# Global attention: latent and context scores of a head in one probability buffer

## Chip, cores and metric

The kernel runs on one core of a Trainium2 chip. The metric is device time in microseconds of one execution, as the median of several. PE is TensorE, DVE is VectorE, ACT is ScalarE, POOL is GpSimd, SP is SyncE. PSUM is the memory that PE writes its products to (eight banks of 512 float32 columns), SBUF the on-chip working memory.

## What is computed

One layer of a backbone over 1024 latent tokens (width 1024) and 256 context tokens. Two attention branches work side by side, each with 8 query heads and 2 key/value heads of 64 columns: a windowed branch (each block of 128 queries sees three blocks of keys, the context, and a sink logit) and a global branch (all 1024 latent keys and the 256 context keys). A gated merge and a convolutional feed-forward part follow. What the change touches is the global branch's softmax:

```python
def _global_attention(q, k_all, v_all):
    ...
    def one_block(i):
        q_blk = lax.dynamic_slice_in_dim(q, i * BLOCK, BLOCK, axis=1)
        p = jax.nn.softmax(_gqa_scores(q_blk, k_all), axis=-1)
        return _gqa_values(p, v_all)
...
o_b = _global_attention(q_b, jnp.concatenate([k_b, k_b_c], axis=1), jnp.concatenate([v_b, v_b_c], axis=1))
```

So each query has one softmax over 1024 + 256 = 1280 keys.

## The kernel before

The attention stage works through 32 **units**. A unit is one branch, one block of 128 queries and one key/value head with its four query heads; units 0 to 15 are windowed, 16 to 31 global. Each unit has *score steps* and, one unit later, *value steps*: while unit u's scores are made, the values of unit u-1 are made. The loop at lines 833 to 863 lays both lists out on a scale from 0 to 1 (the score steps over the first 0.85, the value steps over all of it) and calls them in that order. In units 18 to 25 a third list, *fill*, is spread among them: groups of twelve products of the windowed branch's output projection (`branch_steps`, line 792), each of which takes a transpose slot. This order is that of the source. A list planner then fixes each engine's queue: an earlier instruction goes first, but one whose buffer isn't free yet is passed by later ones that are ready.

A global unit before the change:

- `context`/`cxp` (line 464): PE computes the context scores of all four heads, 4 x 256 columns, into one score buffer. DVE takes their maxima (line 471) and scales them (472). ACT takes four exponentials of 256 columns out of PSUM into one probability buffer `p_x` (line 476, through `soft`, 426).
- `lat(h)` for each head (line 428): four products of 512 columns into a score buffer. One DVE instruction (line 459) scales the 1024 scores, writes them negated to the head's probability buffer and keeps the running minimum, which starts from the context's maximum. ACT takes the exponential in place, with the sum.
- `norm` (line 479): the context exponentials were taken with the context's maximum alone, so they are brought to the common one. DVE forms a difference (483), ACT its exponential (484), POOL multiplies the four slices of `p_x` (487), DVE corrects the sums (488, 489) and takes the reciprocal (494).
- Value steps (line 523): for each of ten key tiles of 128, PE transposes the four heads' 128 columns into one transpose slot (531). ACT writes the rounded high part (`pth`, 540) and DVE the rest (`ptl`, 541), or, for tiles 2 and 6, ACT copies the tile out (537) and POOL splits it (line 538, through 84 and 87). PE then multiplies with the values (552, 553), some tiles later. Key tiles 8 and 9 are the context (`pslice`, 518). The output goes through ACT (558), POOL (560, 566) and DVE (563).
- `qprep` (397) prepares the queries of unit u+2 and `rows` (496) the row of reciprocals; each takes a transpose slot for a short time.

Buffers: two score buffers of two banks (`s_tile`, 765), three transpose slots of one bank (`pt_tile`, 762), one bank for the value sums, and eight probability buffers of 1024 columns (`p_tile`, 768). A windowed unit uses four of the eight, a global unit five. A buffer is free again when the last instruction that reads it is done.

The lines that order the steps, and the loop that places them:

```python
        def score_steps(self):
            steps = [lambda h=h: self.lat(h) for h in range(4)]
            return steps + [self.norm]
...
            steps = [lambda n=n: step(range(n, n + g)) for n in range(0, len(kt), g)]
            steps.insert(2 - self.br, self.rows)
...
        for lst, of, sp in ((ss, 0.0, SPAN[u >= 17]), (vs, VOFF, VSPAN), (fs, 0.0, 1.0)):
            for n, st_ in enumerate(lst):
                seq.append((of + sp * (n + 0.5) / len(lst), st_))
        for _, st_ in sorted(seq, key=lambda e: e[0]):
            st_()
```

Of the kernel before, what the change touches and what calls it, by code (L numbers as in the profile page):

```python
# [13 lines left out]
P = 128  # L14
# [55 lines left out]
def layer_kernel(  # L70
# [313 lines left out]
    class Unit:  # L384
# [43 lines left out]
        def lat(self, h):  # L428
# [29 lines left out]
            p = p_tile(f"p{self.id}_{h}")[:, 0:T if self.br else self.w + NC]  # L458
            nc.vector.tensor_scalar(out=p, in0=o, scalar1=self.qscale(nqs)[:, hs] if self.br else -1.0,  # L459
                                    scalar2=self.other[:, hs], op0=ALU.mult, op1=ALU.min, accum_out=self.nm[:, hs])  # L460
            self.soft(p, p, h, self.nm, self.sm, -1.0)
            self.pc[h, 0] = p

        def cxp(self):
            kh = self.br * 2 + self.g
            s = s_tile(f"s{self.id}_x")
            for h in range(4):
                self.qk(s[:, h * NC:(h + 1) * NC], h, KC[0][:, kh])
            self.other = small(f"nmc_{self.id}", (P, 4))
            self.smc = small(f"smc_{self.id}", (P, 4))  # L470
            nc.vector.reduce_max(self.other, s.rearrange("p (a b) -> p a b", a=4), axis=AX.X)
            nc.vector.tensor_tensor(out=self.other, in0=self.other, in1=self.qscale(nqs), op=ALU.mult)
            p = p_tile(f"p{self.id}_x")
            for h in range(4):
                self.pc[h, 1] = p[:, h * NC:(h + 1) * NC]
                self.soft(s[:, h * NC:(h + 1) * NC], self.pc[h, 1], h, self.other, self.smc,
                          self.qscale(pqs)[:, h:h + 1])

        def norm(self):
            hc = slice(self.g * 4, self.g * 4 + 4)  # L480
            f = small(f"f_{self.id}", (P, 4))
            if self.br:
                nc.vector.tensor_tensor(out=f, in0=self.nm, in1=self.other, op=ALU.subtract)
                nc.scalar.activation(f, f, AF.Exp)
                for h in range(4):
                    p = self.pc[h, 1]
                    nc.gpsimd.tensor_scalar(out=p, in0=p, scalar1=f[:, h:h + 1], scalar2=0.0, op0=ALU.mult, op1=ALU.add)
                nc.vector.tensor_tensor(out=self.smc, in0=self.smc, in1=f, op=ALU.mult)
                nc.vector.tensor_tensor(out=self.sm, in0=self.sm, in1=self.smc, op=ALU.add)
            else:  # L490
# [18 lines left out]
        def score_steps(self):  # L509
            steps = [lambda h=h: self.lat(h) for h in range(4)]  # L510
            return steps + [self.norm]

        def context(self):
            self.begin()
            if self.br:
                self.cxp()
# [1220 lines left out]
```

## Time and profile before

| | us |
|---|---|
| median of the runs shown (3) | 1586.1 |
| lowest and highest | 1586.05 and 1589.05 |
| span of the profiled execution | 1585.4 |
| windowed units, about | 340 to 470 |
| global units, about | 470 to 770 |

The profile is of one execution, and its times count from the start of the span. The span runs from that execution's first instruction to its last and is all that the profile gives of its time; it lies 0.7 us below the median of the runs. Rows of groups read: line, engine, operation, names written and read, shape, count, then busy time in us and the mean of one in ns, then the engine's idle time before them and what ended it. Rows of the timeline read: start in us, length in us, engine, line, operation; a bracket at the end is the engine's idle time before it. A row of waits reads: who waited for whom, us in all, times, longest. Matmul ends are modelled and overlap the next start, so PE's work is better read from the steps between starts.

### The profile page before, as it was taken

How to read it: one execution, taken by the hardware profiler on the slowest of the kernel's cores; microseconds unless marked ns; L12 is line 12 of the kernel's file. 1: busy time of each engine (PE TensorE's matmuls, PEld its weight loads, DVE VectorE, ACT ScalarE, POOL GpSimd, SP SyncE). 2: the span in 40 equal slices, each digit the busy share in tenths (PEclk: the TensorE clock that was granted, in tenths of full speed). 3: DMA queues.
4: the chain of work that ended last, by engine and by line, in shares of the span. 5: the costliest groups of instructions: out<-in, count | busy, mean ns of one | idle time of the engine just before them, and what ended most of it. 6: DMA issues, size and time to landing. Idle time of an engine off the chain costs nothing.

```text
span 1585.4 us, 22064 instructions
## 1 busy us (share of the span) xinstructions
PE 1528.4 (96%) x7680; PEld 1269.8 (80%) x7680; DVE 1195.6 (75%) x1766; ACT 813.0 (51%) x1443; POOL 753.7 (48%) x731
## 2 busy tenths in 40 slices
PE   6999999999999999999999999999999999999996
PEld 5878788878887887777788898888888888888876
DVE  7797646628888777888674779888888877657886
ACT  5422222448887667688531565444444444435642
POOL 0574302426667556665422554666667764021132
PEclk9999999999999999999999999999999999999998
DMA  9695662322236555531451132333334446996721
GB/s 378 217 313 188 221 217 81 120 80 67 62 104 157 139 127 145 118 73 39 142 186 53 60 101 86 114 107 112 115 106 118 111 113 189 358 273 210 255 94 53
DMA packets 112367, 229.98 MB, mean 145 GB/s; under 512 B 12960, under 2 KB 27808, under 8 KB 112160
## 3 DMA queue, kind: packets, MB, share of 16 engines
q1 hardware_dynamic: 96816, 198.93, 37.6%
q0 software_dynamic: 10400, 20.19, 8.2%
q10 hardware_dynamic: 5040, 9.46, 1.6%
q8 instruction: 60, 0.98, 0.3%
q14 instruction: 51, 0.42, 0.1%
HBM read 177.35 MB, written 65.86 MB: 153 GB/s over the span
## 4 chain that ended last, share of the span: by engine, by line
PE 82%; DVE 6%; ACT 4%; issue 3%; POOL 2%; DMA 2%; ACTq 0%; SPq 0%; DVEq 0%; POOLq 0%
PE ptr L531 5%; PE p L90 4%; PE p L91 4%; PE p L92 4%; PE g L90 3%; PE g L91 3%; PE g L92 3%; PE b L92 3%; PE b L91 3%; PE b L90 3%; PE s L414 2%; PE a L92 2%; PE c L91 2%; PE d L91 2%; PE c L92 2%
## 5 line engine op out<-in xcount | busy, mean ns | idle before, releaser
L541 DVE TENSOR_TENSOR ptl<-ptr,pth 128x512 fp32r<-128x512 f32 x188 | 124.8, 685 | 27.5 <-ACT pth L540 25.2
L531 PE MATMUL ptr<-ident,p 128*128 128x128 f32 x816 | 126.5, 278 | 10.3 <-DVE ptl L541 7.8
L540 ACT CAST pth<-ptr 128x512 fp32r<-128x512 f32 x188 | 106.6, 588 | 56.3 <-PE ptr L531 32.7
L87 DVE TENSOR_TENSOR ld<-rd,hd 128x1024 fp32r<-128x1024 f32 x77 | 94.0, 1240 | 52.5 <-ACT hd L82 50.4
L426 ACT ACTIVATE p<-p,nm 128x1024 f32<-128x1024 f32 (+2 forms) x128 | 125.3, 981 | 10.9 <-DVE p L459 10.1
L531 PEld LDWEIGHTS ptr<-ident,p 128*128 128x128 f32 x816 | 93.8, 140 | 40.3 <-DVE ptl L541 13.5
L82 ACT CAST hd<-rd 128x1024 fp32r<-128x1024 f32 x77 | 79.2, 1050 | 81.5 <-PE p L92 50.0
L552 PE MATMUL av<-pth,VT 128*128 128x512 f32 x236 | 104.6, 443 | 1.0 <-ACT avs L558 0.5
L90 PE MATMUL p<-hd 128*128 128x512 f32 x264 | 103.2, 391 | 0.0
L92 PE MATMUL p<-hd,ld 128*128 128x512 f32 x264 | 102.7, 389 | 0.0
L91 PE MATMUL p<-ld,hd 128*128 128x512 f32 x264 | 102.7, 389 | 0.0
L90 PE MATMUL g<-hh,whg 128*128 128x512 f32 x256 | 99.9, 390 | 0.0
L92 PE MATMUL g<-hh,wlg 128*128 128x512 f32 x256 | 99.7, 389 | 0.0
L91 PE MATMUL g<-hl,whg 128*128 128x512 f32 x256 | 99.6, 389 | 0.0
L553 PE MATMUL av<-ptl,VT 128*128 128x512 f32 x236 | 97.6, 414 | 2.0 <-POOL ptl L87 1.9
L87 POOL TENSOR_TENSOR wlg<-wg,whg 128x512 fp32r<-128x512 f32 x32 | 47.0, 1479 | 109.6 <-ACT whg L82 107.3
L459 DVE TENSOR_SCALAR_CACHE_REDUCE p<-s,cvt,nmc 128x1024 f32<-128x1024 f32 x64 | 84.5, 1340 | 12.3 <-PE s L415 11.8
L414 PE MATMUL s<-KL,q 128*128 128x512 f32 (+2 forms) x192 | 76.0, 396 | 2.9 <-ACT p_x L426 2.0
L188 DVE CUSTOM_DVE_ANT_0 wml<-wml,sc,bmc 128x1024 f32<-128x1024 f32 x32 | 45.0, 1416 | 39.0 <-DMA wml<-in_wmodT_dram 38.6
L84 POOL TENSOR_SCALAR pth<-prw 128x512 fp32r<-128x512 f32 x48 | 31.1, 649 | 88.2 <-ACT prw L537 62.7
L82 ACT CAST wS<-s 128x512 fp32r<-128x512 f32 x76 | 45.3, 621 | 52.1 <-POOL s L1079 51.3
L415 PE MATMUL s<-KL,q 128*128 128x512 f32 (+2 forms) x192 | 71.7, 373 | 0.0
(396 smaller groups left out, 4974.0 us busy)
## 6 DMA issues: line engine op xcount, KB each, us to landing
wml<-in_wmodT_dram SPq DMA_DIRECT2D x48, 512.0 KB
ru<-in_w_up_dram SPq DMA_DIRECT2D x38, 512.0 KB
rd<-td SPq DMA_DIRECT2D x55, 256.0 KB
rd<-sd SPq DMA_DIRECT2D x44, 256.0 KB
rd<-in_w_dn_dram SPq DMA_DIRECT2D x33, 256.0 KB
wm<-in_wmodT_dram SPq DMA_DIRECT2D x16, 512.0 KB
wg<-in_w_g_dram SPq DMA_DIRECT2D x32, 256.0 KB
sgd<-sg ACTq DMA_DIRECT2D x32, 256.0 KB
```

The lines of the kernel that those rows point to most:

```text
L82: nc.scalar.copy(hi, src)
L87: lo_eng.tensor_tensor(out=lo, in0=src, in1=hi.bitcast(F32), op=ALU.subtract)
L90: nc.tensor.matmul(ps, a[0], b[0], start=start, stop=False, skip_group_check=resumed)
L91: nc.tensor.matmul(ps, a[0], b[1], start=False, stop=False, skip_group_check=resumed)
L92: nc.tensor.matmul(ps, a[1], b[0], start=False, stop=stop, skip_group_check=resumed)
L414: nc.tensor.matmul(o, self.q[0][:, hs], ks, start=True, stop=False)
L426: nc.scalar.activation(p, s, AF.Exp, bias=nm[:, h:h + 1], scale=scale, accum_out=sm[:, h:h + 1])
L531: nc.tensor.transpose(tr[:, h * P:(h + 1) * P], self.pslice(h, n), ident)
L540: nc.scalar.copy(hi, tr)
L541: nc.vector.tensor_tensor(out=lo, in0=tr, in1=hi.bitcast(F32), op=ALU.subtract)
L552: nc.tensor.matmul(self.av, v, hi, start=first, stop=False)
L553: nc.tensor.matmul(self.av, v, lo, start=False, stop=self.left == 0)
```

## The change

In the global branch the context scores of a head go behind its 1024 latent ones, in a probability buffer of 1280 columns. `cxp` runs twice for a unit, for heads 0 and 1 ahead of the score steps and for heads 2 and 3 between the second head's and the third head's step. Each time it computes two heads' context scores into one transpose slot (instead of a score buffer). For each head a DVE instruction then scales the 256 scores, writes them negated to columns 1024 to 1279 and keeps their minimum. `lat` starts its minimum from that and writes the first 1024 columns, and one exponential of ACT covers all 1280. The rescaling of the context and the correction of the sums go. There are six probability buffers of 1280 columns instead of eight of 1024; a global unit uses four. In the windowed branch two heads share one buffer, 640 columns each, so a unit uses two.

```diff
--- before.py
+++ after.py
@@ -455,39 +455,32 @@
                 self.qk(s[:, 512:512 + NC], h, KC[0][:, kh])
                 o = s[:, 512 - w:512 + NC]
             hs = slice(h, h + 1)
-            p = p_tile(f"p{self.id}_{h}")[:, 0:T if self.br else self.w + NC]
-            nc.vector.tensor_scalar(out=p, in0=o, scalar1=self.qscale(nqs)[:, hs] if self.br else -1.0,
+            if self.br == 0:
+                if h % 2 == 0:
+                    self.pp = p_tile(f"p{self.id}_{h}").rearrange("p (a b) -> p a b", a=2)
+                self.pc[h] = self.pp[:, h % 2, 0:self.w + NC]
+            p = self.pc[h]
+            nc.vector.tensor_scalar(out=p[:, 0:T] if self.br else p, in0=o, scalar1=self.qscale(nqs)[:, hs] if self.br else -1.0,
                                     scalar2=self.other[:, hs], op0=ALU.mult, op1=ALU.min, accum_out=self.nm[:, hs])
             self.soft(p, p, h, self.nm, self.sm, -1.0)
-            self.pc[h, 0] = p
-
-        def cxp(self):
+
+        def cxp(self, a):
             kh = self.br * 2 + self.g
-            s = s_tile(f"s{self.id}_x")
-            for h in range(4):
-                self.qk(s[:, h * NC:(h + 1) * NC], h, KC[0][:, kh])
-            self.other = small(f"nmc_{self.id}", (P, 4))
-            self.smc = small(f"smc_{self.id}", (P, 4))
-            nc.vector.reduce_max(self.other, s.rearrange("p (a b) -> p a b", a=4), axis=AX.X)
-            nc.vector.tensor_tensor(out=self.other, in0=self.other, in1=self.qscale(nqs), op=ALU.mult)
-            p = p_tile(f"p{self.id}_x")
-            for h in range(4):
-                self.pc[h, 1] = p[:, h * NC:(h + 1) * NC]
-                self.soft(s[:, h * NC:(h + 1) * NC], self.pc[h, 1], h, self.other, self.smc,
-                          self.qscale(pqs)[:, h:h + 1])
+            s = pt_tile(f"s{self.id}_x{a}")
+            if a == 0:
+                self.other = small(f"nmc_{self.id}", (P, 4))
+            for h in (a, a + 1):
+                self.qk(s[:, (h - a) * NC:(h - a + 1) * NC], h, KC[0][:, kh])
+            for h in (a, a + 1):
+                p = self.pc[h] = p_tile(f"p{self.id}_{h}")
+                nc.vector.tensor_scalar(out=p[:, T:NK], in0=s[:, (h - a) * NC:(h - a + 1) * NC],
+                                        scalar1=self.qscale(nqs)[:, h:h + 1], scalar2=3.0e38, op0=ALU.mult,
+                                        op1=ALU.min, accum_out=self.other[:, h:h + 1])
 
         def norm(self):
             hc = slice(self.g * 4, self.g * 4 + 4)
-            f = small(f"f_{self.id}", (P, 4))
-            if self.br:
-                nc.vector.tensor_tensor(out=f, in0=self.nm, in1=self.other, op=ALU.subtract)
-                nc.scalar.activation(f, f, AF.Exp)
-                for h in range(4):
-                    p = self.pc[h, 1]
-                    nc.gpsimd.tensor_scalar(out=p, in0=p, scalar1=f[:, h:h + 1], scalar2=0.0, op0=ALU.mult, op1=ALU.add)
-                nc.vector.tensor_tensor(out=self.smc, in0=self.smc, in1=f, op=ALU.mult)
-                nc.vector.tensor_tensor(out=self.sm, in0=self.sm, in1=self.smc, op=ALU.add)
-            else:
+            if self.br == 0:
+                f = small(f"f_{self.id}", (P, 4))
                 nc.vector.tensor_tensor(out=f, in0=self.nm, in1=sinkb[:, hc], op=ALU.add)
                 nc.scalar.activation(f, f, AF.Exp)
                 nc.vector.tensor_tensor(out=self.sm, in0=self.sm, in1=f, op=ALU.add)
@@ -508,17 +501,17 @@
 
         def score_steps(self):
             steps = [lambda h=h: self.lat(h) for h in range(4)]
+            if self.br:
+                steps.insert(2, lambda: self.cxp(2))
             return steps + [self.norm]
 
         def context(self):
             self.begin()
             if self.br:
-                self.cxp()
+                self.cxp(0)
 
         def pslice(self, h, n):
-            if self.br and n >= NT:
-                return self.pc[h, 1][:, (n - NT) * P:(n - NT + 1) * P]
-            return self.pc[h, 0][:, n * P:(n + 1) * P]
+            return self.pc[h][:, n * P:(n + 1) * P]
 
         def value_steps(self):
             nm, kt = self.id, self.kt
@@ -766,7 +759,7 @@
         return ps2.tile([P, T], F32, tag="s", name=name, bufs=2)
 
     def p_tile(name):
-        return att.tile([P, T], F32, tag="p", name=name, bufs=8)
+        return att.tile([P, NK], F32, tag="p", name=name, bufs=6)
 
     def small(name, shape):
         return att.tile(list(shape), F32, tag=name.split("_")[0], name=name,
```

## Prediction, made before the change was run

> **What bounds the kernel now.** I read the page first: its span, its engine totals and PE's share of 40 equal slices.
>
> ```profile
> span 1585.4 us, 22064 instructions
> ...
> PE 1528.4 (96%) x7680; PEld 1269.8 (80%) x7680; DVE 1195.6 (75%) x1766; ACT 813.0 (51%) x1443; POOL 753.7 (48%) x731
> ...
> PE   6999999999999999999999999999999999999996
> ```
>
> PE is busy for 96% of the span, and for nine tenths or more of every slice but the first and the last. So an engine beside it matters only where PE waits for it. The change touches the attention stage, so next come the busy times by stretch, cut where a global unit opens. The maximum at line 471 marks that: 16 units, numbered 16 to 31; the rows of the timeline below are those of units 19, 26 and 31.
>
> ```profile
> L471 DVE TENSOR_REDUCE nmc<-s_x x16: 1209/1215/1226, 472.5 to 747.7; 128x4 f32<-128x1024 f32 x16
> ```
>
> ```profile
> 521.61 1.22 DVE L471 TENSOR_REDUCE nmc<-s_x 128x4 f32<-128x1024 f32 x1
> ...
> 665.86 1.22 DVE L471 TENSOR_REDUCE nmc<-s_x 128x4 f32<-128x1024 f32 x1
> ...
> 747.74 1.22 DVE L471 TENSOR_REDUCE nmc<-s_x 128x4 f32<-128x1024 f32 x1
> ```
>
> The busy times by stretch give the length, then the busy microseconds of PE, PE's weight loads, DVE, ACT and POOL:
>
> ```profile
> 472.46:521.61 49.15, 45.52 (x258) 35.65 (x257) 40.38 (x74) 39.34 (x90) 33.98 (x49) 1.00 0.73 171
> 521.61:665.86 144.25, 141.53 (x795) 116.06 (x794) 106.41 (x183) 96.74 (x210) 83.59 (x111) 1.00 0.56 132
> 665.86:764.00 98.14, 90.96 (x533) 72.13 (x531) 86.27 (x146) 80.20 (x180) 57.61 (x83) 1.00 0.23 54
> ```
>
> Units 19 to 25 carry "fill" (the output projection of the windowed branch): 144.25 / 7 = 20.6 us a unit, and PE idles 2.72 us in all, 0.4 a unit. The units from 26 have no fill: (747.74 - 665.86) / 5 = 16.4 us each, and PE idles 98.14 - 90.96 = 7.18 us in six, 1.2 a unit. With the first stretch that makes 13.5 us of idle PE in 291.5. This caps what relief of other engines can give here. What PE waited for in it:
>
> ```profile
> PE ptr L531 <- DVE ptl L541: 7.1, 11, 1.6
> PE s L414 <- ACT p_x L426: 2.0, 3, 0.8
> ```
>
> PE is as full after this stage, so I pass a shift of the stage on to the span in full.
>
> **What goes and what comes, engine by engine.** These groups are the durations that I use.
>
> ```profile
> L459 DVE TENSOR_SCALAR_CACHE_REDUCE p<-s,cvt,nmc 128x1024 f32<-128x1024 f32 x64 | 84.5, 1340 | 12.3 <-PE s L415 11.8
> ...
> L426 ACT ACTIVATE p<-p,nm 128x1024 f32<-128x1024 f32 x64 | 73.8, 1154 | 8.9 <-DVE p L459 8.2
> ...
> L426 ACT ACTIVATE p_x<-s_x,nmc,cvt 128x256 f32<-128x256 f32 x64 | 35.4, 567 | 4.9 <-DVE nmc L472 4.9
> ...
> L487 POOL TENSOR_SCALAR p_x<-p_x,f 128x256 f32<-128x256 f32 x64 | 29.9, 497 | 10.2 <-ACT f L484 10.1
> ...
> L426 ACT ACTIVATE p<-p,nm 128x640 f32<-128x640 f32 x28 | 23.4, 839 | 0.0
> L459 DVE TENSOR_SCALAR_CACHE_REDUCE p<-s,negsink 128x640 f32<-128x640 f32 x27 | 23.1, 874 | 0.2 <-PE s L415 0.2
> ...
> L483 DVE TENSOR_TENSOR f<-nm,nmc 128x4 f32<-128x4 f32 x16 | 7.1, 446 | 0.1
> ...
> L459 DVE TENSOR_SCALAR_CACHE_REDUCE p<-s,negsink 128x512 f32<-128x512 f32 x8 | 5.6, 742 | 0.0
> ...
> L489 DVE TENSOR_TENSOR sm<-sm,smc 128x4 f32<-128x4 f32 x16 | 5.6, 353 | 0.1
> ...
> L488 DVE TENSOR_TENSOR smc<-smc,f 128x4 f32<-128x4 f32 x16 | 4.9, 306 | 2.5 <-ACT f L484 2.5
> ...
> L472 DVE TENSOR_TENSOR nmc<-nmc,cvt 128x4 f32<-128x4 f32 x16 | 4.6, 289 | 0.2
> ```
>
> DVE loses, per unit, the maximum (1.215) and four small operations (0.289 + 0.446 + 0.306 + 0.353): 2.6 us. It gains four reductions of 256 columns out of PSUM, a form that the trace does not have. The 512- and 640-column rows differ by 132 ns for 128 columns, 1.03 ns a column; 742 - 256 x 1.03 = 0.48 us each, as an estimate. The bounds are 0.43 (with the 1.21 ns a column between the 640 and 1024 rows) and the whole 742 of the 512-column row. I take 0.48, since 512 is the nearest row: +1.9, net **-0.7 us a unit** (-0.9 to +0.4).
>
> ACT loses four small exponentials (2.3) and gains 256 columns on each of four large ones. The slope from 640 to 1024 columns is (1154 - 839) / 384 = 0.82 ns, so 0.21 us each, 1364 ns for the new form: net **-1.4 us a unit**. POOL loses the four rescalings, **-2.0**. PE's own work stays: the same eight context products, now in two lots of four. No DMA is issued, removed or moved.
>
> Nothing of this is PE time. The exponential of the context held one of two score buffers; the 2.0 us that PE waited for it go. Of the 7.1 us for DVE's `ptl` I take 1.5, since DVE only loses 0.7 of some 14.4 us a unit (86.27 / 6); the bounds are 0 and 7.1.
>
> Relief in sum: 2.0 + 1.5 = **-3.5 us**, with bounds of 0 and -9.1.
>
> How sure DVE's share is depends on its small operations, which are uneven:
>
> ```profile
> 667.11 2.22 DVE L472 TENSOR_TENSOR nmc<-nmc,cvt 128x4 f32<-128x4 f32 x1
> ```
>
> ```profile
> 666.92 2.40 POOL L87 TENSOR_TENSOR lwb<-rwb,hwb 128x1024 fp32r<-128x1024 f32 x1
> ```
>
> Four elements took 2.22 us while POOL ran a 2.40 us operation. The Trainium skill (SBUF — State Buffer, section "SBUF: two separate sides") says that VectorE and GpSimd share a port pair under an exclusive lock, and that a VectorE operation with two SBUF inputs is blocked for a whole GpSimd instruction; this row agrees. By that rule such stalls leave with the instructions, because the new reductions have one PSUM input, and DVE's net stays at -0.7; if the stalls were chance and moved to DVE's next instruction, the net would be about half of that and the relief nearer -2.8.
>
> **What the change makes wait.** The probabilities lie in a ring of buffers. Before, a unit used five of eight (four heads, one for the context of all). Unit u's first three went in beside the five of unit u-1, and its third and fourth heads needed a head buffer of u-1 back, which the transposes of key tiles 0 to 7 release. The trace shows this hand-over in unit 31:
>
> ```profile
> 757.61 0.60 PE L531 MATMUL ptr<-ident,p 128*128 128x128 f32 x4
> ...
> 757.92 1.34 DVE L459 TENSOR_SCALAR_CACHE_REDUCE p<-s,cvt,nmc 128x1024 f32<-128x1024 f32 x1
> ...
> 759.19 1.34 DVE L459 TENSOR_SCALAR_CACHE_REDUCE p<-s,cvt,nmc 128x1024 f32<-128x1024 f32 x1
> ...
> 759.21 1.03 PE L531 MATMUL ptr<-ident,p_x 128*128 128x128 f32 x8
> ...
> 760.92 1.15 ACT L426 ACTIVATE p<-p,nm 128x1024 f32<-128x1024 f32 x1
> ...
> 762.05 0.83 PE L531 MATMUL ptr<-ident,p 128*128 128x128 f32 x5
> ```
>
> Transposes of tile 7 at 757.61; the third head's reduction 0.3 us later and the fourth behind it; the fourth exponential at 760.92; the next unit's transposes that read it at 762.05, some 4.1 us after the release. In between PE has the transposes of the context tiles (1.03) and products of values and of the next scores, so it hardly idles.
>
> After, a unit uses four of six. The third and fourth heads again wait for u-1, but a buffer now also holds the context columns, which are transposed last (key tiles 8 and 9). So the release comes after **all** transposes of u-1. What follows on DVE and ACT, from the release: two context reductions (2 x 0.40, the busy time less the 0.08 by which the next one starts early), two large ones (2 x 1.27, the step from 757.92 to 759.19), and the last exponential behind the one before it (1.36, and 0.3 for hand-overs): **5.0 us** until the next unit's transposes can finish their first tile. Queued behind those four reductions on DVE are the `ptl` of tiles 8 and 9 and the next unit's first reductions, and PE's value products wait for them.
>
> What PE has to do in these 5 us is priced by the steps from one start to the next: context products, a head's four score products (to the transposes behind them), and value products.
>
> ```profile
> 746.73 0.28 PE L414 MATMUL s_x<-KC,q 128*128 128x256 f32 x1
> 746.84 0.28 PE L415 MATMUL s_x<-KC,q 128*128 128x256 f32 x1
> ...
> 756.03 0.39 PE L414 MATMUL s<-KL,q 128*128 128x512 f32 x1
> ...
> 756.94 0.60 PE L531 MATMUL ptr<-ident,p 128*128 128x128 f32 x4
> ...
> 758.28 0.40 PE L552 MATMUL av<-pth,VT 128*128 128x512 f32 x1
> 758.52 0.40 PE L553 MATMUL av<-ptl,VT 128*128 128x512 f32 x1
> ```
>
> Value products of four tiles are left, 8 x 0.24 = 1.9; the first two heads' context, 4 x 0.12 = 0.5; two heads' scores, 2 x 0.91 = 1.8, each only when DVE has read a score buffer. That is 4.2 us. The gap is 0.8 a unit. Fill groups come too late in the order to cover it and need a transpose slot. Part of the gap falls into the 0.4 to 1.2 us that PE idles already; I take 0.5 for each of 15 units (17 to 31): **+7.5 us**, with bounds of 0 and 15 x 0.9 = +13.5.
>
> Second, the context scores leave the score buffers for the three transpose slots (`pt_tile`). The lot for heads 2 and 3 is computed early (ahead of key tiles 2 and 3) but is only read after the release, so one of three slots is blocked for most of the value tiles. A slot's life is the transposes (0.60 for four, above) and what reads it:
>
> ```profile
> L541 DVE TENSOR_TENSOR ptl<-ptr,pth 128x512 fp32r<-128x512 f32 x167 | 111.0, 685 | 27.4 <-ACT pth L540 25.2 <-POOL O L87 0.8 <-PE av L553 0.5
> ...
> L540 ACT CAST pth<-ptr 128x512 fp32r<-128x512 f32 x164 | 93.2, 588 | 53.1 <-PE ptr L531 29.8 <-PE av L552 20.8
> ```
>
> That is 1.9 us (0.60 + 0.59 + 0.69), and with the queues on ACT and DVE some 2.6, as an estimate. A tile whose split POOL does needs ACT alone, 1.2, and so does the query tile. For key tiles 2 to 9 through two slots that makes (6 x 2.6 + 3 x 1.2) / 2 = 9.6 us. With 0.9 for tiles 0 and 1 (1.03 for eight transposes in the rows above, less the tail) and the 5.0 above, a unit without fill can't be shorter than 15.5. It takes 16.4 now, so I book nothing, but the margin is only 0.9.
>
> Windowed units: two heads share a buffer, six hold twelve heads instead of eight. DVE lost 0.2 us there on scores and nothing on buffers, so I book nothing. If waits went by buffer rather than by columns, each odd head would wait 0.84 us for the even one's exponential, at most 64 / 2 x 0.84 = 27 us; the heads' columns don't overlap, so I leave that out of the range.
>
> Sum: -3.5 + 7.5 = +4.0; span 1589.4. The median of the runs, 1586.1, is 0.7 above the profiled span, so I predict **1590.1 us**.
>
> **Rivals.** *Slots and buffers starve PE (slower by far).* The margin of 0.9 us goes where a slot's life passes 2.9 us, since each 0.1 of life costs 6 x 0.1 / 2 = 0.3 us a unit. At 3.3 a unit takes 17.6, +1.2 in 15 units: +18 us, and +8 to +25 for lives about that. For it: PE waited longest for `ptl` even with three free slots. Against it: ACT and POOL get lighter, and these feed the slots. The Trainium skill (Perfetto Trace Analysis, section "Optimization Strategy") names this case: a gap that repeats through a stretch can mean that the next tile finds no SBUF or PSUM. No run here shows it yet; before, PE idles 0.4 us in a unit with fill.
>
> *The relief wins (faster).* If the list order puts five us of PE work between the release and the next transposes, the chain is hidden as it is now; only the relief stays: -3.5 to -9.1 us, 1577 to 1583, with 1580 in its middle. It decides where at least 0.8 us of products of older tiles or of fill are left at the release. For it: in the hand-over quoted PE hardly idles over 4.1 us. Against it: with fill, PE has only 0.4 us a unit to win back.
>
> *Both cancel.* Within 2 us of before, since PE's own work is the same.
>
> **How the numbers follow.** Forecast (+0.5 to +8, with 0.5 a unit booked for a gap of 0 to 0.9): 0.42. Starved: 0.18. Relief wins: 0.30. Cancel: 0.10. About 0.2% (3.2 us) is what a measurement here can tell from none. Slower by more: 0.27 of the forecast and all of the starved case, 0.45. Faster by more: 0.30. The rest, 0.25, is within it. The range reaches from 1578 (most of the relief case) to 1603 (the starved case but for its end).
>
> **What would show it.** Right: a new DVE form of 128x256 near 0.48 us x64, an ACT form of 128x1280 near 1.36 us, no POOL rescaling; third-head reductions behind the last transposes of u-1; units from 26 on at 16 to 17 us and a PE gap ahead of each unit's first transposes. Wrong: these reductions ahead of the last transposes, or PE waiting for `ptl` by over 15 us in the stage (starved), or PE idle below 10 us in it (relief).

## Result, and the profile after

The change makes the kernel slower: 1609.45 us (four runs, 1607.65 to 1611.09) beside 1586.09 before, a ratio of 1.0132 with an interval of 1.0112 to 1.0152. That is +23.4 us by the medians where +4.0 was forecast, and above the range; by the ratio, which the experiments below go by, it is +20.9 (0.0132 x 1586.1). The direction was right; the time is that of the rival "Slots and buffers starve PE".

Single operations came out as worked out. The page of the changed kernel, its span, totals, PE's slices and groups:

```profile
span 1609.3 us, 21848 instructions
...
PE 1541.5 (96%) x7680; PEld 1267.9 (79%) x7680; DVE 1193.0 (74%) x1814; ACT 792.8 (49%) x1299; POOL 724.1 (45%) x667
...
PE   6999999999999999999899999999999999999996
```

Two groups of it, with shapes kept apart:

```profile
L426 ACT ACTIVATE p<-p,nm 128x1280 f32<-128x1280 f32 x64 | 87.3, 1365 | 26.2 <-DVE p L463 26.0
...
L476 DVE TENSOR_SCALAR_CACHE_REDUCE p<-s_x,cvt 128x256 f32<-128x256 f32 x64 | 28.9, 473 | 10.0 <-PE ptr L524 10.0
```

The long exponential takes 1365 ns (1364 forecast), the reduction of 256 columns 473 ns (480 forecast). POOL loses 29.6 us of 753.7, ACT 20 of 813, DVE only 2.6 of 1195.6. Every engine but PE has less to do, and PE's 7680 products are the same in number. Yet ACT's exponentials now wait 26 us for DVE instead of 8, and DVE's context reductions 10 us for PE's transposes, which are read as the release. One slice of PE falls from 9 to 8.

Busy times by stretch, cut as before (length, then busy PE, weight loads, DVE, ACT, POOL):

```profile
473.13:525.59 52.46, 49.10 (x268) 36.71 (x266) 39.46 (x81) 34.76 (x59) 28.34 (x37) 1.00 0.67 161
525.59:684.46 158.87, 147.56 (x795) 113.69 (x792) 104.36 (x204) 87.16 (x148) 73.97 (x85) 1.00 0.51 121
684.46:785.00 100.54, 92.02 (x522) 69.00 (x520) 81.67 (x163) 72.44 (x125) 43.51 (x56) 1.00 0.22 51
```

The units with fill (second row) take 158.87 / 7 = 22.7 us instead of 20.6. PE idles 11.3 us in that stretch instead of 2.7, and its "busy" time grew by 6 with the same 795 products, since ends are modelled: lengths say more than busy times here. The last value product moved from 774.26 to 797.67, by 23.4 us, and what follows it is as long as before (811.1 and 811.6 us). So the loss lies in the attention stage. Cut from one first-head reduction to another in both kernels, units 19 to 25 take 158.9 us instead of 143.1 (2.3 more each), units 26 to 30, which have no fill, 83.7 instead of 80.6 (0.6 more each), and the last unit up to its last value product 5.3 more.

What PE waited for in all of it, which was 7.1 us for `ptl` and 2.0 for `p_x` before:

```profile
PE s L414 <- DVE p L463: 6.6, 14, 0.6
PE av L546 <- POOL ptl L87: 3.7, 6, 1.2
PE ptr L524 <- DVE ptl L534: 3.2, 9, 0.9
PE ptr L524 <- ACT p L426: 2.0, 1, 2.0
```

The wait for `p_x` is gone and the one for `ptl` is less than half. What has grown most: PE's score products wait 14 times, 6.6 us in all, for a score buffer that DVE has not read; before, once for 0.5 us. This names who ended a wait, not why that engine was late. The reason shows in the timeline of one unit with fill; first PE, from the transposes ahead of the release on:

```profile
608.12 0.60 PE L524 MATMUL ptr<-ident,p 128*128 128x128 f32 x4
608.80 0.50 PE L90 MATMUL b<-O,hwb 128*128 128x512 f32 x1
...
611.42 0.39 PE L92 MATMUL b<-O,lwb 128*128 128x512 f32 x1
...
612.72 1.04 PE L524 MATMUL ptr<-ident,p 128*128 128x128 f32 x8
...
615.69 0.50 PE L414 MATMUL s<-KL,q 128*128 128x512 f32 x1 [0.53 <-DVE p L463]
...
618.54 0.74 PE L524 MATMUL ptr<-ident,p 128*128 128x128 f32 x5
...
623.07 0.28 PE L414 MATMUL s_x<-KC,q 128*128 128x256 f32 x1
```

And DVE:

```profile
611.86 0.69 DVE L808 TENSOR_TENSOR bT<-b,bT 128x512 f32<-128x512 f32 x1 [1.72 <-PE b L92]
...
613.47 0.48 DVE L476 TENSOR_SCALAR_CACHE_REDUCE p<-s_x,cvt 128x256 f32<-128x256 f32 x1 [0.92 <-PE ptr L524]
...
613.88 0.48 DVE L476 TENSOR_SCALAR_CACHE_REDUCE p<-s_x,cvt 128x256 f32<-128x256 f32 x1
...
614.28 1.34 DVE L463 TENSOR_SCALAR_CACHE_REDUCE p<-s,cvt,nmc 128x1024 f32<-128x1024 f32 x1
...
615.55 1.34 DVE L463 TENSOR_SCALAR_CACHE_REDUCE p<-s,cvt,nmc 128x1024 f32<-128x1024 f32 x1
...
616.81 1.28 DVE L534 TENSOR_TENSOR ptl<-ptr,pth 128x512 fp32r<-128x512 f32 x2
618.01 0.47 DVE L476 TENSOR_SCALAR_CACHE_REDUCE p<-s_x,cvt 128x256 f32<-128x256 f32 x1
...
618.60 0.45 DVE L476 TENSOR_SCALAR_CACHE_REDUCE p<-s_x,cvt 128x256 f32<-128x256 f32 x1
...
634.04 0.48 DVE L476 TENSOR_SCALAR_CACHE_REDUCE p<-s_x,cvt 128x256 f32<-128x256 f32 x1 [1.47 <-PE ptr L524]
```

ACT's two exponentials behind them:

```profile
615.67 1.36 ACT L426 ACTIVATE p<-p,nm 128x1280 f32<-128x1280 f32 x1 [1.24 <-DVE p L463]
...
617.03 1.35 ACT L426 ACTIVATE p<-p,nm 128x1280 f32<-128x1280 f32 x1
```

Three things are to be seen. The third head's chain does start behind the last transposes (612.72, then 613.47), as forecast. And the next unit's lot of heads 2 and 3, computed at 623.07, is first read at 634.04: it holds one of three transpose slots for 11 us of a unit of some 21. (From its first product to the end of its last read it is 11.9 to 16.6 us in units 19 to 25 and 8.7 to 11.1 from unit 26 on.) Ahead of the release a fill group takes one of the two that are left (its products from 608.80, its read on DVE at 611.86 for 0.69 us), and the last transposes come only then, 4.6 us after the ones at 608.12; PE works almost without a pause in these 4.6 us, so what is late is the release. Last, at the hand-over all three slots are taken: the two tiles transposed at 612.72 keep theirs until DVE has made their `ptl` behind the four reductions (616.81 to 618.09), and the next unit's first lot, computed at 614.52, keeps the third until 619.05, 4.5 us. PE's next transposes start at 617.76.

### The profile page after: what moved, and what is told of

The parts are those of the page before. It is cut to its first block, busy times and chain, and to the rows that moved or that the text cites. A ratio compares the mean times of both kernels' runs of the same rounds, so it can differ in the third digit from the quotient of the medians.

```text
span 1609.3 us, 21848 instructions
## 1 busy us (share of the span) xinstructions
PE 1541.5 (96%) x7680; PEld 1267.9 (79%) x7680; DVE 1193.0 (74%) x1814; ACT 792.8 (49%) x1299; POOL 724.1 (45%) x667
## 4 chain that ended last, share of the span: by engine, by line
PE 74%; DVE 8%; DMA 6%; issue 4%; POOL 3%; ACT 3%; SPq 0%; ACTq 0%; POOLq 0%; DVEq 0%
PE ptr L524 5%; PE p L92 4%; PE p L91 4%; PE p L90 4%; PE b L90 3%; PE b L92 3%; PE b L91 3%; PE g L90 2%; PE g L91 2%; PE g L92 2%; DVE p L463 2%; DMA wml<-in_wmodT_dram 2%; PE c L90 2%; PE d L90 2%; PE a L90 2%
## 5 line engine op out<-in xcount | busy, mean ns | idle before, releaser
L524 PE MATMUL ptr<-ident,p 128*128 128x128 f32 x944 | 151.2, 281 | 8.6 <-DVE ptl L534 3.9
L426 ACT ACTIVATE p<-p,nm 128x1280 f32<-128x1280 f32 (+2 forms) x128 | 138.8, 1087 | 28.1 <-DVE p L463 27.8
L524 PEld LDWEIGHTS ptr<-ident,p 128*128 128x128 f32 x944 | 110.6, 142 | 48.0 <-DVE ptl L534 10.2
L414 PE MATMUL s<-KL,q 128*128 128x512 f32 (+2 forms) x192 | 79.3, 413 | 8.1 <-DVE p L463 6.6
L415 PE MATMUL s<-KL,q 128*128 128x512 f32 (+2 forms) x192 | 73.0, 380 | 0.0
```

What stands on the lines that cost most here:

```text
L426: nc.scalar.activation(p, s, AF.Exp, bias=nm[:, h:h + 1], scale=scale, accum_out=sm[:, h:h + 1])
L524: nc.tensor.transpose(tr[:, h * P:(h + 1) * P], self.pslice(h, n), ident)
```

## Experiments

Theory, after the result: the slot that the lot of heads 2 and 3 holds costs most. "The release" is the end of the last transposes of unit u-1, which frees the buffer that the third head needs. Rivals: the late release alone, or fill groups that the order puts ahead of the last transposes. A ratio is to the kernel before, run on the same chip; times in us from it are taken times 1586.1. Each run's trace also gives the length of the attention stage, from the first windowed reduction on DVE to the last value product; before it is 428.2 us and after 450.5 (+22.3). Pieces of it (units 19 to 25, for example) run from one first-head reduction to another. They are good to some 3 us only, since a fill group, 12 products of 0.23 us, can fall on either side of a cut.

**One maximum in the buffers of before** (`before_onemax`): the relief without the new buffers. The context scores stay in a score buffer and `p_x`; four reductions replace maximum and scaling, the exponential of the context follows with the common maximum, and the rescaling goes.

```diff
             self.soft(p, p, h, self.nm, self.sm, -1.0)
+            if self.br:
+                self.soft(self.pc[h, 1], self.pc[h, 1], h, self.nm, self.smc, -1.0)
...
+                nc.vector.tensor_scalar(out=self.pc[h, 1], in0=s[:, h * NC:(h + 1) * NC],
+                                        scalar1=self.qscale(nqs)[:, h:h + 1], scalar2=3.0e38, op0=ALU.mult,
+                                        op1=ALU.min, accum_out=self.other[:, h:h + 1])
```

> A version that takes the change's good part alone: the kernel before with its buffers (context of all heads in one buffer, one score buffer for the lot), but the context scores are scaled by four DVE reductions, the latent minimum starts from them, and the context's exponentials use the common maximum, so that POOL's rescaling and most small operations go. No slot is taken and no release moves. The relief of the prediction alone: -3.5 us (0 to -9.1), 1577 to 1587. If DVE's longer hold on the score buffer counts more, 1587 to 1592.

Measured: 1585.59 beside 1588.75, ratio 0.9980 (0.9971 to 0.9989), -3.2 us; stage 425.5. The relief is real, of the size booked (-3.5), and this kernel is faster than both. One maximum is not what costs.

**Context scores of heads 2 and 3 out of the slot at once** (`after_landing`): scaled into a buffer of their own in SBUF as soon as they are computed, and carried into the probability buffers by POOL after the release.

```diff
+            if a:
+                land = att.tile([P, 2, NC], F32, tag="land", name=f"land{self.id}", bufs=1)
...
+                p = None if a else p_tile(f"p{self.id}_{h}")
+                o = land[:, h - a] if a else p[:, T:NK]
...
+            for h in (a, a + 1) if a else ():
+                p = self.pc[h] = p_tile(f"p{self.id}_{h}")
+                nc.gpsimd.tensor_scalar(out=p[:, T:NK], in0=land[:, h - a], scalar1=1.0, scalar2=0.0,
+                                        op0=ALU.mult, op1=ALU.add)
```

> The changed kernel, but the context scores of heads 2 and 3 are first scaled into a small buffer of their own (2 x 256 columns, one of them), and POOL copies them into the probability buffers when these come free. The transposes' slot is free again at once, and the two context reductions leave the chain behind the release (5.0 us becomes about 4.2); the release itself stays behind all transposes of the unit before. If the blocked slot is the cause, nearly all of the 23 us goes: 1586 to 1594. If the late release is the cause, only the 0.8 us a unit goes, 8 to 12 us: 1597 to 1602.

Measured: 1593.73, ratio 1.0027 (1.0014 to 1.0040), +4.3; stage 433.3. The lot in a unit with fill, on PE, and its last read on DVE:

```profile
614.02 0.28 PE L414 MATMUL s_x<-KC,q 128*128 128x256 f32 x1
```

```profile
615.23 0.48 DVE L479 TENSOR_SCALAR_CACHE_REDUCE land<-s_x,cvt 128x256 f32<-128x256 f32 x1
```

The slot is held for 1.7 us instead of 11. So 17 of the 21 to 23 us go. Three things changed at once, though: the slot is free early, two reductions leave DVE's chain behind the release, and POOL enters it. ACT's long exponentials now wait for POOL's copies too, 12.7 us in all, which they don't in the changed kernel:

```profile
L426 ACT ACTIVATE p<-p,nm 128x1280 f32<-128x1280 f32 x64 | 87.3, 1365 | 23.3 <-POOL p L485 12.7 <-DVE p L463 10.4
```

In seven of the 16 units (17, 19, 23, 25 to 28) the copies stand behind other work of POOL and the third head's exponential starts 2.2 to 4.1 us after the start of the last transposes, in most others some 1.5.

**The same with DVE's copies** (`after_landing_dve`): the carrying is put back into DVE's chain.

```diff
-                nc.gpsimd.tensor_scalar(out=p[:, T:NK], in0=land[:, h - a], scalar1=1.0, scalar2=0.0,
-                                        op0=ALU.mult, op1=ALU.add)
+                nc.vector.tensor_copy(p[:, T:NK], land[:, h - a])
```

> As after_landing (the transposes' slot of heads 2 and 3 is free early), but DVE copies the 2 x 256 columns into the probability buffers, so that the chain behind the release keeps two small DVE steps. Slot theory: within 4 us of after_landing, 1590 to 1598. If after_landing gained from the shorter DVE chain instead, 8 to 12 us come back: 1600 to 1606.

Measured: 1598.09, ratio 1.0056 (1.0041 to 1.0071), +8.9; stage 437.2. The group of copies in its trace:

```profile
L485 DVE COPY p<-land 128x256 f32<-128x256 f32 x32 | 15.2, 515 | 7.3 <-PE ptr L531 7.3
```

At 515 ns each on average the copies are no shorter than the reductions (473) that they stand for, and the release is as late as in the changed kernel. What still differs in the main is the slot: 20.9 - 8.9 = 12.0 us by ratios, 450.5 - 437.2 = 13.3 us by the stage.

**The slot held, alone, and its control** (`after_landing_hold`, `after_landing_free`). To price the hold with nothing else, one small DVE instruction is added to `after_landing`, at the place where the third head's buffer is free. In one kernel it reads a column of the slot, in the other a column of the buffer in SBUF; later work overwrites what it writes.

```diff
                 p = self.pc[h] = p_tile(f"p{self.id}_{h}")
+                if h == a:
+                    nc.vector.tensor_copy(p[:, 0:1], s[:, 0:1])
```

In the control the last line is:

```diff
+                    nc.vector.tensor_copy(p[:, 0:1], land[:, 0, 0:1])
```

> As after_landing, with one small DVE instruction a global unit added: once the third head's probability buffer is free, it copies one column of the transpose slot that holds the context scores of heads 2 and 3 into that buffer (the column is overwritten afterwards). The scores themselves have been read long before; the instruction only keeps the slot taken until the release, as in the changed kernel. If the held slot is what the changed kernel loses, this returns most of the loss: 10 to 15 us over after_landing, 1603 to 1609. If the loss lies in the reductions behind the release, it stays within 4 us of after_landing (1590 to 1598).

> The control of after_landing_hold: the same small instruction at the same place, but it reads the column from the buffer in SBUF that the scores were moved to, so the slot is free early. By every theory within 3 us of after_landing (1590 to 1597); what after_landing_hold takes beyond this is the price of the held slot alone.

Measured: 1608.09, ratio 1.0122 (1.0098 to 1.0145), for the hold; 1600.55, 1.0064 (1.0047 to 1.0081), for the control. The added instruction in the control's groups, and then in those of the hold:

```profile
L486 DVE COPY p<-land 128x1 f32<-128x1 f32 x16 | 2.4, 152 | 4.9 <-PE ptr L534 4.9
```

```profile
L486 DVE COPY p<-s_x 128x1 f32<-128x1 f32 x16 | 2.5, 158 | 10.0 <-PE ptr L534 10.0
```

The same instruction with the same length, but with the slot held the transposes that it waits for come later: 10.0 us of idle DVE ahead of it instead of 4.9. The hold costs 1608.09 - 1600.55 = 7.5 us (9.7 by the stage, 449.1 against 439.4). Units 19 to 25 and 26 to 30 of the control, and then of the kernel with the hold:

```profile
523.09:676.18 153.09, 142.10 (x794) 115.28 (x793) 105.34 (x211) 87.48 (x147) 79.37 (x99) 1.00 0.54 125
676.18:759.58 83.40, 76.50 (x442) 60.27 (x441) 69.24 (x143) 60.56 (x104) 40.68 (x58) 0.98 0.26 59
```

```profile
524.43:682.88 158.45, 147.70 (x794) 113.98 (x793) 104.94 (x212) 87.41 (x149) 79.06 (x99) 1.00 0.52 121
682.88:766.62 83.74, 77.97 (x442) 58.85 (x440) 68.24 (x140) 60.31 (x103) 40.94 (x58) 1.00 0.25 59
```

With the hold they take 158.45 us, as in the changed kernel (158.88 between the same marks), with 794 products in both rows; with the slot free 153.09. That is 5.4 of the loss; the rest lies ahead of unit 19 and in the last unit. Units 26 to 30 hold the slot for 8.3 to 10.4 us each and lose 0.3 us by it in all: in this pair the held slot costs where fill asks for slots too. (The order of each engine's queue is planned again for each kernel, so the price includes what the planner makes of the held slot.)

The control missed its own expectation: 16 instructions of 0.15 us cost 1.0064 - 1.0027, 5.9 us, or 0.37 us for each. More than the instruction differs in its trace. Unit 27 of `after_landing`, POOL's two copies and the third head's exponential on ACT:

```profile
704.31 0.77 POOL L485 TENSOR_SCALAR p<-land 128x256 f32<-128x256 f32 x2
```

```profile
704.75 1.37 ACT L426 ACTIVATE p<-p,nm 128x1280 f32<-128x1280 f32 x1 [1.10 <-POOL p L485]
```

The same in the control:

```profile
707.84 0.78 POOL L487 TENSOR_SCALAR p<-land 128x256 f32<-128x256 f32 x2
```

```profile
708.66 1.37 ACT L426 ACTIVATE p<-p,nm 128x1280 f32<-128x1280 f32 x1 [1.49 <-POOL p L487]
```

Without the instruction the exponential starts behind the first copy, with it behind the second. Over the units in which POOL's copies come late, these exponentials start 2.6 us later in all than in `after_landing`; with 16 x 0.15 = 2.4 us for the instructions that makes 5.0 of the 5.9, as an estimate. So the 5.9 us are not the price of a longer chain on DVE alone.

**Late release in the buffers of before** (`before_late`, `onemax_late`): key tiles in the order 0 to 3, 8, 9, 4 to 7, so that head buffers come free behind all transposes; no slot is used. The second does it to `before_onemax`.

```diff
-                self.kt = list(range(10))
+                self.kt = [0, 1, 2, 3, 8, 9, 4, 5, 6, 7]
...
+            n = self.kt[n] if self.br else n
```

> The kernel before, but global units transpose their key tiles in the order 0 to 3, 8, 9, 4 to 7, with the context in the middle. Slots, DVE, ACT and POOL work stay; only the buffers of heads 2 and 3 come free behind all ten tiles instead of eight, as in the changed kernel. If the late release is the cause, this costs about 1 us a unit: 1594 to 1606. If the blocked slot is the cause, the time stays: 1584 to 1589.

> before_onemax with the key tiles taken in the order 0 to 3, 8, 9, 4 to 7, so that the head buffers come free behind all transposes, as in the changed kernel, with no slot used. If the late release costs the 9 us that before_late cost, the time is 1593 to 1597. If a lighter DVE, ACT and POOL hide part of it, as the prediction booked, it is 1587 to 1592; the loss then lies in units 26 to 31 and not in those with fill.

Measured: 1597.38, ratio 1.0054 (1.0039 to 1.0070), +8.6, and 1592.02, ratio 1.0022 (1.0010 to 1.0033), +3.5, which is 6.7 over `before_onemax`; by the stage +9.0 and +5.0. Both expectations leave out that in this order the third head takes the buffer of `p_x`, which is free after key tile 9, the third of five pairs. A stretch of `before_late`, DVE:

```profile
685.38 1.34 DVE L459 TENSOR_SCALAR_CACHE_REDUCE p<-s,cvt,nmc 128x1024 f32<-128x1024 f32 x1
...
689.39 1.34 DVE L459 TENSOR_SCALAR_CACHE_REDUCE p<-s,cvt,nmc 128x1024 f32<-128x1024 f32 x1 [1.46 <-PE ptr L532]
```

The third head's reduction runs 4.0 us ahead of the fourth's, where the changed kernel has them 1.3 us apart. That the third head has `p_x`'s buffer is read from this order; the trace doesn't name buffers. So these two price a late release of one head's buffer, 5 to 9 us, of which units 19 to 25 lose only 1.3 and 0.8, and units 26 to 30 3.9 and 2.8; that of both heads without any slot was not tried.

**Short use of slots** (`onemax_slots`): `before_onemax` with its context products in two slots, two heads at a time, read at once.

```diff
-            s = s_tile(f"s{self.id}_x")
-            for h in range(4):
-                self.qk(s[:, h * NC:(h + 1) * NC], h, KC[0][:, kh])
+            s = pt_tile(f"s{self.id}_x{a}")
+            for h in (a, a + 1):
+                self.qk(s[:, (h - a) * NC:(h - a + 1) * NC], h, KC[0][:, kh])
```

> before_onemax (kernel before with one maximum, separate context buffer, two exponentials a head, no rescaling; 3.2 us faster than before) with its context products in two transpose slots, two heads at a time, read at once, since the release of the probability buffers is early here. If any use of a slot in the units with fill costs, units 19 to 25 rise from 145 to 149 us or more and the time is 4 to 9 us over before_onemax. If only a slot held for long costs, it is within 2 us of before_onemax (1584 to 1588).

Measured: 1592.32, ratio 1.0019 (1.0009 to 1.0029), +3.0, which is 6.2 over `before_onemax` (4.7 by the stage). So even two short uses cost. But not where it was expected: units 19 to 25 take 143.8 us (145.1 without slots), units 26 to 30 80.2 instead of 76.6, and the last one 4.8 more. The first lot holds its slot for 1.9 us here (median) and for 4.5 in the changed kernel, so this is no exact price of the changed kernel's first lot.

**No slot in the changed kernel's order** (`after_landing_s`): `after_landing` with the products of all four heads in one score buffer.

```diff
+                s = self.sx = s_tile(f"s{self.id}_x")
+                for h in range(4):
+                    self.qk(s[:, h * NC:(h + 1) * NC], h, KC[0][:, kh])
```

> As after_landing (the scaled context scores of heads 2 and 3 go to a buffer of their own and GpSimd carries them over), but the context products of all four heads go into one score buffer, as before the change, and no transpose slot is used for them. Left of the change: late release of the probability buffers, one exponential a head, no rescaling. If even the short use of two slots a unit is what after_landing still loses in the units with fill (150.7 us there for units 19 to 25 against 143.1 before), these units come back to 143 to 146 us and the time lies at before or up to 5 us under it (1584 to 1590). If after_landing's rest is the late release, it stays at 1590 to 1596 with 149 to 152 us in those units.

Measured: 1599.35, ratio 1.0065 (1.0046 to 1.0085), +10.3, slower than with slots and outside both expectations; stage 435.2 against 433.3. A score buffer is no cheaper a place. It also moves four reductions to the head of the unit, so it prices no single term, and 3.3 of its 10.3 us lie outside the stage and stay unexplained.

**The lot late** (`after_late_lot`): in the changed kernel, the lot and the scores of heads 2 and 3 behind the last key tiles.

```diff
-                seq.append((of + sp * (n + 0.5) / len(lst), st_))
+                seq.append((0.93 + 0.01 * n if lst is ss and u > 16 and n in (3, 4, 5, 6) and u < nu
+                            else of + sp * (n + 0.5) / len(lst), st_))
```

> The changed kernel with the context lot and the score steps of heads 2 and 3 (and the norm) placed behind the last key tiles in the order. The lot then takes a slot only when no key tile waits for one; the release stays behind all transposes, and the chain behind it grows by about 0.6 us a unit. Slot theory: most of the 23 us comes back, 1588 to 1598. Release theory: nothing or a loss, 1606 to 1618.

Measured: 1610.80, ratio 1.0135 (1.0120 to 1.0150). Units 19 to 25 gain 3.6 us (155.3) and units 26 to 30 lose 3.2 (86.9): the slot is spared (the lot now holds it for 1.6 to 2.1 us in these units), but the products of two heads now stand in the chain behind the release. The time lies in the range of the rival, the late release, and not in the 1588 to 1598 of the slot's theory, which had priced the longer chain at 0.6 us a unit. Sparing the slot this way gains nothing; whether the longer chain takes all of the gain back is not shown.

**Fill behind the last key tiles** (`after_fill_last`, `before_fill_last`).

```diff
-        for lst, of, sp in ((ss, 0.0, SPAN[u >= 17]), (vs, VOFF, VSPAN), (fs, 0.0, 1.0)):
+        for lst, of, sp in ((ss, 0.0, SPAN[u >= 17]), (vs, VOFF, VSPAN), (fs, 0.93, 0.02)):
```

> The changed kernel with the fill groups of a unit all behind the last key tiles of the value steps, so that PE has them in the stretch between the release and the next unit's transposes. If the late release with a fill group in front of it is the cause, most of the 14.6 us that units 19 to 25 lost comes back: 1594 to 1600. If the blocked slot is the cause, fill still needs the two slots that are left: 1605 to 1613.

> Control: the same move of the fill groups in the kernel before. The release there comes ahead of the last two key tiles, which cover it already, so both theories expect little: 1583 to 1590.

Measured: 1608.77, ratio 1.0119 (1.0093 to 1.0144), and 1595.08, ratio 1.0035 (1.0022 to 1.0048). Fill that stands at the release doesn't bring the loss back: 2 us gained in the changed kernel, within the intervals, and 5.6 lost in the one before. The range of the release theory, 1594 to 1600, is missed. But the control shows that the move itself has a price, which neither expectation had; if it is the same in both kernels, fill at the release is worth some 2.0 + 5.6 = 7.6 us in the changed one, as an estimate. So the late release is not the whole loss, and it may well be a part of it.

**Two slots for all** (`before_two_slots`): the kernel before with one transpose slot less, in all units.

```diff
-        return ps2.tile([P, 512], dt, tag="pt", name=name, bufs=3)
+        return ps2.tile([P, 512], dt, tag="pt", name=name, bufs=2)
```

> The kernel before with two transpose slots instead of three, in windowed and global units: the price of a slot that is never there. Slot theory: at least the 15 us or so that it ascribes to a slot blocked for part of each global unit, 1602 to 1640. If slots don't bind, within 5 us: 1584 to 1592.

Measured: 1624.54, ratio 1.0220 (1.0203 to 1.0237), +34.9; stage 466.7, of whose 38.5 the windowed units lose 17.7 and the global ones 20.8. One slot less for the whole of each global unit costs some 21 us, then; one held for 11 of 21 us would cost about half of that, as a rough estimate, and the pair above measured 7.5 to 9.7. Unit by unit this doesn't hold: units 19 to 25 lose 4.0 of the 20.8 here, less than the 5.4 by the hold alone, and units 26 to 30 lose 5.5. What a slot is worth depends on the order around it.

The steps that lead from one kernel to the other, each beside the one before it:

| from the kernel before to | us against before (by ratio) | step | stage |
|---|---|---|---|
| one maximum, buffers of before | -3.2 | relief -3.2 | 425.5 |
| `after_landing` | +4.3 | late release, short use of slots, waits for POOL's copies +7.5 | 433.3 |
| `after_landing_free` | +10.2 | one more instruction in the chain, and later waits for POOL +5.9 | 439.4 |
| `after_landing_hold` | +19.4 | slot held +9.2 | 449.1 |
| the change | +20.9 | two reductions on DVE for the instruction and POOL's copies +1.5 | 450.5 |

The last step is within the intervals of both. No run prices the late release of both heads' buffers alone; more probability buffers in place of six, which would take it away, were not tried.

## Why the prediction was wrong

- **What bounds the kernel: right.** PE bounds the stage, and with the same products the loss is PE waiting in it: in the three rows of busy times its idle time grows from 13.5 to 23.2 us, and the rest of the 20.3 us hides in busy times, whose ends are modelled.
- **Durations: right**, 1365 and 473 ns for 1364 and 480; **DVE's net only half right.** In the global units DVE's busy time falls from 236.7 to 230.6 us, 0.4 a unit and not 0.7, since the output's additions (`ot<-avs,up`, two operands in SBUF) now take 28.5 us there instead of 24.3. That fits the case which the prediction weighed and didn't take, that stalls move to other instructions. The rule of the Trainium skill weighed there (SBUF — State Buffer, section "SBUF: two separate sides") has an operation with two SBUF inputs blocked while a GpSimd instruction holds the port pair. For the new reductions, which read PSUM, the trace agrees: all 64 lie between 451 and 485 ns.
- **Relief, -3.5: right**, measured alone at -3.2 (-4.6 to -1.7).
- **Late release, +7.5: right in kind; its size was not measured alone.** The hand-over is as described: from the third head's first reduction (613.47) it takes 3.6 us to the fourth exponential (617.03) and 5.1 to the transposes that read it (618.54), for 5.0 forecast. The nearest prices are 5 to 9 us for one head's buffer, and 7.5 for release, short use of slots and POOL's copies together. Units 26 to 30, at 16.7 us each within the 16 to 17 forecast, lose 0.6 a unit, about the 0.5 booked; the loss beyond it lies in units 19 to 25 and in the last one.
- **Slots, 0: this step failed.** "It takes 16.4 now, so I book nothing, but the margin is only 0.9." The margin was made from the bound of a unit *without* fill, with slot lives that start when PE is ready for them. In the units with fill, some two groups a unit also take slots: the one quoted from 608.80 to 612.55 (its read on DVE ends there), 3.75 us. Added to the prediction's own terms that makes 9.6 + 0.9 + 5.0 + 2 x 3.75 / 2 = 19.3 us, as an estimate, beside 20.6 of a unit that PE fills: a margin of 1.3 us in which everything would have to fit without a wait. And the slot's life of "some 2.6" was too low. Matched in order, the key tiles that DVE reads hold a slot for 3.3 us on average in the changed kernel (3.5 before), tiles 8 and 9 for 4.6 and 4.8, since their `ptl` stands behind the four reductions. The first two heads' lot, 4.5 us, was not in the budget at all. By the prediction's own rule the margin goes at 2.9. The rule is no sound bound either: for 3.3 it gives 17.6 us for a unit without fill, which takes 16.7. The runs put the held slot at 7.5 to 13 us and the short use of two at 5 to 6, in place of nothing. Not all of the loss is priced: of the 15.8 us that units 19 to 25 lose, the pair puts 5.4 down to the held slot, and `after_landing`, without it, still loses 7.7 there; how these divide among release, first lot and POOL's copies stays open.
- **The 5.0 us chain, priced by its gap to PE's work: not settled.** "I take 0.5" for a unit supposed that PE's idle time absorbs part of the gap. A 0.15 us instruction in the chain came with 0.37 us a unit, about half of it from POOL's copies; two copies of 0.5 us each, in `after_landing_dve`, came with 0.29 a unit, but without POOL. Neither is the chain's price alone.
- **The cover: half right.** "Fill groups come too late in the order to cover it": in the unit shown one runs ahead of the last transposes, another at 620.21 behind the chain. Put at the release by hand, they gained 2 us of 23, some 7.6 against the control.
- **Rivals and signs.** The rival of starving slots had the mechanism and a range (+8 to +25) that holds the result; its sign, a PE waiting for `ptl` by over 15 us, did not come (3.2 and 3.7 for POOL's). PE waits for `s`, `ptl`, `rb` and `p` in small parts, as would be so if a slot that is taken delays whatever asks next; the list of waits alone doesn't show the slot. The claim for it that was weighed against PE's 0.4 us of idle a unit, that a gap which repeats can mean a lack of PSUM (the Trainium skill, Perfetto Trace Analysis, section "Optimization Strategy"), agrees with the pair of hold and control, where a held slot alone costs 7.5 us. "The relief wins" needed the buffers of before.

## What to carry to other kernels

A buffer's cost is the time from its first write to its last read, not the work done in it: before moving a product into a smaller ring, look for the latest thing that its reader needs, here a buffer that another unit frees last. Make the slot budget for the fullest unit, with all that asks for a slot in it and with lives read from the trace, waits included, and treat a margin of a few per cent as spent. To take the gain without the loss, split the change: one maximum with the old buffers gave -3.2 us, while the one exponential for 1280 columns, which needed the shared buffers, cost over 20.

## What the runs showed of the hardware

Copies of 256 columns from SBUF to SBUF on DVE were uneven, where the reductions of as many columns out of PSUM were steady. Shortest, median and longest in ns, with the first and last start, of the copies in `after_landing_dve` and then of the reductions in the changed kernel:

```profile
L485 DVE COPY p<-land x32: 280/371/1593, 480.1 to 768.5; 128x256 f32<-128x256 f32 x32
```

```profile
L476 DVE TENSOR_SCALAR_CACHE_REDUCE p<-s_x,cvt x64: 451/477/485, 473.1 to 780.7; 128x256 f32<-128x256 f32 x64
```

The slowest pair of copies, on DVE:

```profile
686.30 1.79 DVE L485 COPY p<-land 128x256 f32<-128x256 f32 x2 [0.50 <-PE ptr L531]
```

And on POOL in the same stretch:

```profile
685.16 1.52 POOL L87 TENSOR_TENSOR ptl<-prw,pth 128x512 fp32r<-128x512 f32 x1
686.41 0.96 POOL L87 TENSOR_TENSOR O<-ot,O 128x256 fp32r<-128x256 f32 x1
```

POOL's spans are rough, but the split is clear: the 13 copies beside which no POOL operation runs take 280 to 291 ns, the 19 that overlap one take 280 to 1593 ns, 673 on average. Carrying data on DVE from SBUF to SBUF is no cheap way out of a slot while POOL is at work.
